# A triangular inverse kept in two shared PSUM banks, and GpSimd adding the squares of six row tiles

## The chip, the cores and the metric

The kernel runs on one core of a Trainium2 chip. The metric is the device time of one execution in microseconds (us). Each version is timed in several executions and the median is reported. One further execution is recorded by the hardware profiler; the line numbers, durations and waits below come from that one.

The engines of the core work side by side, each through its own fixed list of instructions, and wait for one another by semaphores: TensorE (PE, the matmuls; its weight loads are shown as PEld), VectorE (DVE), ScalarE (ACT), GpSimd (POOL) and SyncE (SP, which issues the DMAs). Operands lie in SBUF, or in PSUM, which the matmuls write.

## The reference

One inference step of a decoder with two layers, for a prompt of 512 tokens and 8 samples of 4 tokens, 544 token columns in all, at a model width of 1024. Layer 0 mixes tokens by dilated window attention, layer 1 by an RWKV-7 recurrence; both also attend to 256 memory tokens, are gated and go through an output projection. What matters here is layer 1:

```python
def step(S, inp):
    r_t, w_t, k_t, v_t, a_t, b_t = inp
    sa = jnp.einsum('bhvk,bhk->bhv', S, a_t)
    S = S * w_t[:, :, None, :] + sa[..., None] * b_t[:, :, None, :] + v_t[..., None] * k_t[:, :, None, :]
    return S, jnp.einsum('bhvk,bhk->bhv', S, r_t)
...
h = jnp.concatenate([y, o_mem], axis=-1) * jax.nn.silu(gate)
return h @ w_out, cols[:, -1], S.astype(xn.dtype)
...
xp = xp + rms_norm(hp, norm_post[i])
```

There are 12 heads of 64 channels. The last line, an RMS norm over the 1024 channels of the projection's output, is the end of the program: it needs the sum of the squares of all eight row tiles (8 x 128 channels).

## The kernel before, in words

**The recurrence in chunks.** The kernel takes the 512 prompt tokens in 8 chunks of 64. Heads go in pairs (six pairs p), and two pairs make a group g (three groups, 0 to 2). For each pair, coroutines called `decay`, `keys`, `receptance`, `values` and `scores` compute the scaled vectors and the masked score matrices (tiles `SA`, `SR`). For each group follow three serial steps:

- `products(g)` inverts, for each of 32 (head, chunk) units, a unit triangular 64x64 matrix. It is cut in 32x32 blocks; DVE lays them out so that each of the 128 partitions holds one 32x32 block, by a transpose into the SBUF tile `TT` (L1354), writes ones on the diagonal (L1355), and eliminates in 30 steps s = 1 to 30 (L1377 to L1382). Each step is two DVE instructions on s x (31-s) elements per partition: a product into the SBUF tile `TX` (L1380), and an addition of it into `TT` in place (L1382). The elements of a step depend on those of the step before. Two small squarings (after steps 5 and 12) serve the samples' small chunks. Then `TT` is transposed into `TX` (L1390), PE makes the off-diagonal blocks (tiles `X`, L1396 and L1405, with a second transpose at L1397 between them), and then the products called w, q and v.
- `recur(g)` runs the chain over the eight chunks. Its states and its z products lie in a PSUM tile that `ps_zs` gives out: 128 partitions x 1024 words, two banks, one buffer. The chain's last state is `St_7`, and it reports `end{g}` when done with the tile. The cross attention of layer 1 uses the same two banks ahead of group 0 and reports `cross`.
- `norm` and `sample` normalise the outputs y and treat the samples.

So the backbone of layer 1 is elimination, X, w/q/v, chain, then the next group's elimination. Beside it runs other work that fills the engines: the input projection of later pairs (PE matmuls `b_h`, three per product of high and low parts of the split numbers, L301 to L303), the splitting of weights (ACT `hi_...` L293, POOL `lo_...` L294), the gates (`u`, `gt`, L1131 to L1133), and the output projection (`outer`, PE matmuls `o`, with the gated vectors `ug` split into `h`, L1688 to L1690).

**The end.** `last(0)` and `last(1)` finish the projection for the 256 columns and the 288 columns of the tokens. For each of eight row tiles they run six matmuls, add them to `z` (DVE, L1722), square z (ACT, L1724, tiles `sqo`), and have PE sum the squares over partitions by products with a column of ones (`add_squares`, L316, tile `ssz`). Then comes the reciprocal root (L328 to L343, whose result for part 0 is `rs_p`), the scaling of z (L1733), the addition of the residual `xr` (L1734; three tiles on DVE, five on POOL), and the store.

**What sets the order.** Each stage is a coroutine; its `yield`s carry estimated times, or the name of an event that it must wait for. A small event queue in the kernel (`flow`) runs the coroutines in the order that these estimates and ranks give, and the framework's list scheduler then settles the order of every engine's instructions from a simulated timeline. A `yield` more, an instruction more or a buffer less moves the order of everything behind it. The list of each engine is then fixed.

```python
def add_squares(acc, sq, n, first, last): ...      # PE, L316
RADD = (0, 3, 6)                                   # rows whose residual DVE adds
LAT = [4.0, 5.82, 0.4, 0.6, 5.42, 5.2, 1.5, 0.94, 2.61, 0.6]
RANK = [4, 2, 7, 3, 2, 4, 6, 9]
```

Of the kernel before, what the change touches and what calls it, by code (L numbers as in the profile page):

```python
# [16 lines left out]
ALU = mybir.AluOpType  # L17
# [11 lines left out]
RAWO = 4  # L29
XRB = 8  # L30
OFF = {0: 0, 8: 0, 9: -200, 10: -200}
RADD = (0, 3, 6)
ET = mybir.EngineType
D, A, G = ET.DVE, ET.Activation, ET.Pool
# [134 lines left out]
class Flow:  # L169
# [29 lines left out]
    def run(self):  # L199
        while self.streams:  # L200
            s = self.pick()
            try:
                with self.tc.high_priority(OFF[s.rank]) if OFF.get(s.rank) else ExitStack():
                    r = next(s.gen)
# [21 lines left out]
def _device(tc, I, O):  # L226
    nc = tc.nc
# [31 lines left out]
    def ps_zs(name):  # L259
        return psum[0].tile([128, 1024], F32, tag="zs", bufs=1, name=name)  # L260
# [51 lines left out]
    def add_squares(acc, sq, n, first, last):  # L312

        for i in (0, 256, 128) if n > 256 else (0, 128):
            w = min(128, n - i)
            nc.tensor.matmul(acc[0:w, i // 128:i // 128 + 1], sq[:, i:i + w], ones[:, 0:1],  # L316
                             start=first and i == 0, stop=last and i == 128)
# [124 lines left out]
    with ExitStack() as pro:  # L442
        pm = pool(pro, "x", 1)
        for h in range(2):
            x = [pm.tile([128, 4, HF], F32, name=f"x{h}{i}") for i in range(2)]
            sq = []
# [24 lines left out]
        for h in range(2):  # L471
            acc = ps_q(f"ss0{h}")
# [181 lines left out]
    with ExitStack() as pro:  # L654
# [14 lines left out]
        for h in range(4):  # L669
            t = bd[h:h + 1, :]  # L670
# [203 lines left out]
    u = pb_pool.tile([128, 4, NT], F32, tag="PB", bufs=1, name="u0")  # L874
# [29 lines left out]
    def bank(h):  # L904
        return ps_c("so", "ssz1") if h else ps_o("ssz0")

    acc, rp, wo, wide, sums, lates, ready = [bank(0), bank(1)], [None, None], [], [], [], [], {}
# [434 lines left out]
    def products(g):  # L1342
# [7 lines left out]
        TT = rw.tile([128, 32, 32], F32, tag="TT", bufs=1, name=f"TT{g}")  # L1350
        TX = rw.tile([128, 32, 32], F32, tag="TX", bufs=1, name=f"TX{g}")
        N_ = SA[:, 0].rearrange("p j (c b t) -> p (j c) b t", b=2, t=32)
        flat = TX.rearrange("p u t -> p (u t)")
        nc.vector.transpose(TT.rearrange("p j t -> p t j"), N_.rearrange("p u b t -> p t b u"))  # L1354
        nc.vector.memset(TT.rearrange("p s t -> p (s t)")[:, 0:1024:33], 1.0)  # L1355

        ts = flat[:, 512:704].rearrange("p (k j t) -> p k j t", k=3, j=2)
        nc.vector.transpose(ts[:, 0], SAs)
        for r in Q0:
# [17 lines left out]
        for s in range(1, 31):  # L1377
            w = 31 - s
            pd = flat[:, 0:s * w].rearrange("p (j t) -> p j t", t=w)
            nc.vector.tensor_tensor(pd, TT[:, s:s + 1, s + 1:32].to_broadcast([128, s, w]),  # L1380
                                    TT[:, 0:s, s:s + 1].to_broadcast([128, s, w]), ALU.mult)
            nc.vector.tensor_tensor(TT[:, 0:s, s + 1:32], TT[:, 0:s, s + 1:32], pd, ALU.add)  # L1382
            if s in (5, 12):
                yield 0.0, LAT[9]
                square(s // 12)
                yield 0.2, LAT[9]
            else:
                yield 0.0, LAT[9]

        nc.vector.transpose(TX.rearrange("p u s -> p s u"), TT)  # L1390
        yield 0.0, LAT[6]

        pt = ps_q(f"X{g}1")
        for u in range(16):
            for a, b in zip(Q0, Q1):
                nc.tensor.matmul(pt[b, 32 * u:32 * u + 32], N_[a, u, 1], TX[a, u], start=True, stop=True)  # L1396
        nc.vector.transpose(N_.rearrange("p u b t -> p t b u"), TT.rearrange("p j t -> p t j"))  # L1397
        for hh, b in enumerate(Q1):
            nc.gpsimd.memset(N_[b, :, 0], 0.0)
            both[hh](TX[b, 0:16], pt[b].rearrange("p (u t) -> p u t", t=32))  # L1400
# [21 lines left out]
        u = st.u = UV[:, 0].rearrange("p j (c e v) -> p (j c) e v", c=4, e=2)  # L1422
# [278 lines left out]
    def last(i):  # L1701

        n, ts = (256, 288)[i], PART[i]
        z, h1 = out.z[i], out.h1
        t, xr = by_row(i, "SA", 2048, "xr1")
        m = 7 + (not i)
        nc.sync.dma_start(t[:, 0:m * n].rearrange("p (k t) -> p k t", t=n), x1d[:, 0:m, ts])
        if i:
            nc.sync.dma_start(xr[7], x1d[:, 7, ts])
        for j in (4, 5):  # L1710
            gated(j, (i,))
        yield 0.0, 2.0
        zs = ps_zs("ssz11") if i else None
        acc = zs[:, 0:512] if i else ps_t("ssz10")
        sqs = []
        for mt in range(8):
            ps = ps_mm(f"o2{mt}{i}")
            for k in range(2):
                a = (mt % 2 * 2 + k) * 128
                mm1(ps, out.w2h[:, mt // 2, a:a + 128], out.w2l[:, mt // 2, a:a + 128],  # L1720
                    h1[:, 0, 4 + k, ts], h1[:, 1, 4 + k, ts], n, k == 0, k == 1)
            nc.vector.tensor_tensor(z[mt], z[mt], ps[:, :n], ALU.add)  # L1722
            sq = tmp(f"sqo1{mt}{i}")[:, 0:n]
            nc.scalar.activation(sq, z[mt], AF.Square)  # L1724
            sqs.append(sq)
            if mt:
                add_squares(acc, sqs[mt - 1], n, mt == 1, False)
            yield 0.75, 0.2
        add_squares(acc, sqs[7], n, False, True)
        rp = rstd_of(acc, n, lambda name: zs[:, 512:1024] if i else ps_t(name), f"p1{i}")  # L1730
        yield 0.2, 2.0
        for kt in range(8):
            nc.vector.scalar_tensor_tensor(z[kt], z[kt], vec("post1", kt), rp, ALU.mult, ALU.mult)  # L1733
            (nc.vector if kt in RADD else nc.gpsimd).tensor_tensor(z[kt], z[kt], xr[kt], ALU.add)  # L1734
            nc.sync.dma_start(O["y"][:, kt, ts], z[kt])
            yield 0.0, 0.7
# [128 lines left out]
```

## Time and profile before

| what | value |
|---|---|
| median of 3 runs | 885.98 us (885.35 to 887.4) |
| the profiled execution | 886.03 us, of which the span from the first to the last instruction is 884.2 us |
| mean granted TensorE clock | 0.94 of full speed |
| PE / DVE / ACT / POOL busy | 91% / 60% / 34% / 39% of the span |
| elimination of group 0, 1, 2 (first L1380 to L1390) | 495.5 to 547.2, 612.9 to 663.7, 731.7 to 776.0 us |
| last chain state `St_7` of group 0, 1, 2 | 615.1, 727.7, 837.9 us |
| last matmul of `last(1)`'s sums of squares ends | 872.2 us |

A row of the timeline reads: start, duration, engine, line, operation, output <- inputs, shape (partitions x elements per partition), and how many alike follow each other (xN). A bracket gives the idle time before it and whose result ended it. The grouped view has, after the bar, the total busy time and the mean in ns. In the stretches view each engine's busy time in us is followed by its number of instructions, and PEclk is the clock that the throttle granted. The trace counts an fp32 matmul of sums (L316) as two instructions where the program has one.

### The profile page before, as it was taken

The page shows a single profiled execution, that of the slowest core. Times are in us where ns is not written, and L with a number is a line of the kernel's source. Part 1 is how long each engine was busy: PE and PEld are TensorE (multiplying, and loading weights), DVE is VectorE, ACT ScalarE, POOL GpSimd, SP SyncE. Part 2 cuts the span into 40 slices and gives each one's busy share as a digit, 9 for nine tenths or more (in the row PEclk, how much of TensorE's full clock was granted, in tenths as well). Part 3 has the DMA queues.
Part 4 walks back from the last instruction along what each step waited for, and adds up shares of the span by engine and source line. Part 5 has one row for each costly group of instructions (what it writes and reads, how often), then busy time and mean ns, then how long its engine had stood idle before and what let it go on. Part 6 is the DMA issues. An engine that isn't in the chain of part 4 may idle for free.

```text
span 884.2 us, 19847 instructions
## 1 busy us (share of the span) xinstructions
PE 805.3 (91%) x8144; PEld 685.6 (78%) x8144; DVE 529.5 (60%) x1189; ACT 304.9 (34%) x657; POOL 346.4 (39%) x426
## 2 busy tenths in 40 slices
PE   5799999999999988899999997998899898599984
PEld 4688777868876758898888876887688787389884
DVE  6534321256276356665775999567997569942563
ACT  6324321233254244455452343322433123222220
POOL 3543213311220335455542455353554344534432
PEclk9999999999999989899999998999999999589975
DMA  5461285672211664343133321201122212422011
GB/s 208 132 225 61 96 288 193 220 259 74 73 62 68 237 217 150 107 163 107 49 98 129 113 66 51 75 27 52 60 78 75 86 60 92 129 69 97 29 55 53
DMA packets 58510, 99.09 MB, mean 112 GB/s; under 512 B 6351, under 2 KB 24047, under 8 KB 58383
## 3 DMA queue, kind: packets, MB, share of 16 engines
q1 hardware_dynamic: 58420, 97.83, 33.5%
q8 instruction: 64, 1.05, 0.5%
q14 instruction: 26, 0.21, 0.1%
HBM read 83.76 MB, written 14.05 MB: 111 GB/s over the span
## 4 chain that ended last, share of the span: by engine, by line
PE 68%; DVE 19%; issue 5%; ACT 3%; DMA 2%; POOL 2%; DVEq 0%; SPq 0%; ACTq 0%; POOLq 0%
DVE TT L1382 3%; DVE TX L1380 3%; PE o L301 2%; PE o L302 2%; PE o L303 2%; PE o L746 2%; PE sc L1312 2%; PE so L830 2%; PE sA L775 1%; PE y L1566 1%; PE b_h L301 1%; PE z L1566 1%; PE pa L738 1%; PE b_h L302 1%; PE ssz L316 1%
## 5 line engine op out<-in xcount | busy, mean ns | idle before, releaser
L294 POOL TENSOR_TENSOR lo_a<-raw_a,hi_a 128x512 fp32r<-128x512 f32 x46 | 60.0, 1304 | 138.7 <-ACT hi_a L293 137.4
L294 POOL TENSOR_TENSOR lo_b<-raw_b,hi_b 128x512 fp32r<-128x512 f32 x58 | 77.3, 1334 | 59.4 <-ACT hi_b L293 54.2
L293 ACT CAST hi_b<-raw_b 128x512 fp32r<-128x512 f32 x58 | 35.8, 618 | 80.4 <-PE b_h L303 26.3
L293 ACT CAST hi_a<-raw_a 128x512 fp32r<-128x512 f32 x48 | 29.7, 619 | 67.2 <-issue 13.5
L301 PE MATMUL b_h<-xg,hi_b 128*128 128x272 f32 x160 | 48.8, 312 | 3.6 <-DVE C L1072 3.1
L303 PE MATMUL b_h<-xg,hi_b 128*128 128x272 f32 x160 | 47.2, 300 | 0.0
L302 PE MATMUL b_h<-xg,lo_b 128*128 128x272 f32 x160 | 47.1, 299 | 0.0
L1380 DVE TENSOR_TENSOR TX<-TT 128x30 f32<-128x30 f32 (+14 forms) x90 | 44.7, 497 | 1.7
L1382 DVE TENSOR_TENSOR TT<-TT,TX 128x30 f32<-128x30 f32 (+14 forms) x90 | 42.4, 471 | 1.7
L301 PEld LDWEIGHTS b_h<-xg,hi_b 128*128 128x128 f32 x160 | 31.0, 196 | 6.7 <-DVE C L1072 3.8
L303 PEld LDWEIGHTS b_h<-xg,hi_b 128*128 128x128 f32 x160 | 31.0, 194 | 1.0 <-issue 0.8
L302 PEld LDWEIGHTS b_h<-xg,lo_b 128*128 128x128 f32 x160 | 31.0, 195 | 0.8 <-issue 0.5
L1312 PE MATMUL sc<-AR,BK 64*64 64x128 f32 x384 | 26.9, 276 | 0.0
L301 PE MATMUL o<-h,hi_o1a 128*128 128x256 f32 (+1 forms) x64 | 20.1, 326 | 3.8 <-ACT h L1689 3.8
L1312 PEld LDWEIGHTS sc<-AR,BK 64*64 64x64 f32 x384 | 20.5, 133 | 3.1 <-issue 1.2
L1608 POOL TENSOR_TENSOR Sd<-St,DF 128x128 f32<-128x128 f32 x21 | 9.8, 468 | 32.6 <-DVE St L1624 31.7
L303 PE MATMUL o<-h,hi_o1a 128*128 128x256 f32 (+1 forms) x64 | 19.8, 324 | 1.3 <-POOL h L1690 1.3
L302 PE MATMUL o<-h,lo_o1a 128*128 128x256 f32 (+1 forms) x64 | 19.7, 320 | 0.0
L723 ACT ACTIVATE P<-P,m 128x768 f32<-128x768 f32 x16 | 15.0, 937 | 12.0 <-DVE m L722 11.9
L1221 POOL TENSOR_TENSOR rv<-rv,mhalf 128x10 f32<-128x10 f32 x6 | 11.8, 1959 | 18.2 <-DVE rv L1220 18.2
L301 PE MATMUL o<-h,hi_o1b 128*128 128x256 f32 (+1 forms) x32 | 11.4, 355 | 8.3 <-ACT h L1689 5.4
L746 PE MATMUL o<-PT,vt 128*64 128x128 f32 x192 | 17.6, 283 | 0.5 <-ACT PT L739 0.5
(915 smaller groups left out, 2869.6 us busy)
## 6 DMA issues: line engine op xcount, KB each, us to landing
raw_b<-in_w_in_b SPq DMA_DIRECT2D x58, 256.0 KB, 2.6
raw_a<-in_w_in_a SPq DMA_DIRECT2D x48, 256.0 KB, 2.7
kc<-in_kc SPq DMA_DIRECT2D x18, 512.0 KB, 5.2
vc<-in_vc SPq DMA_DIRECT2D x18, 512.0 KB, 4.7
out_win<-t SPq DMA_DIRECT2D x12, 272.0 KB, 2.1
PB<-bd SPq DMA_DIRECT2D x4, 576.0 KB, 7.2
x<-in_x SPq DMA_DIRECT2D x4, 544.0 KB, 6.0
xr<-in_x SPq DMA_DIRECT2D x16, 136.0 KB, 2.7
```

What stands on the lines that cost most here:

```text
L293: nc.scalar.copy(hi, raw)
L294: lo_eng.tensor_tensor(lo, raw, hi.bitcast(F32), ALU.subtract)
L301: nc.tensor.matmul(ps[:, :n], hi, xh, start=first, stop=False)
L302: nc.tensor.matmul(ps[:, :n], lo, xh, start=False, stop=False)
L303: nc.tensor.matmul(ps[:, :n], hi, xl, start=False, stop=last)
L723: nc.scalar.activation(P, P, AF.Exp, bias=m1[:, 0:1], scale=1.0, accum_out=m1[:, 1:2])
L746: nc.tensor.matmul(po[64 * hh:64 * hh + 64, 0:128], v, PT[hh][:, j, :], start=j == 0, stop=j == 5)
L830: nc.tensor.matmul(po[QD[b4], 0:256], PT[:, 4 * j + k, QD[b4]], vc[b4][:, k, :], start=j + k == 0, stop=False)
L1312: nc.tensor.matmul(pt[unit(c, j, h)[0], a:a + 128], BK[H2[h], j, x, CH[c]], AR[H2[h], j, :, CH[c]], start=True, stop=True)
L1380: nc.vector.tensor_tensor(pd, TT[:, s:s + 1, s + 1:32].to_broadcast([128, s, w]), TT[:, 0:s, s:s + 1].to_broadcast([128, s, w]), ALU.mult)
L1382: nc.vector.tensor_tensor(TT[:, 0:s, s + 1:32], TT[:, 0:s, s + 1:32], pd, ALU.add)
L1566: nc.tensor.matmul(out, lhs, rhs, start=start, stop=stop)
```

## The change

Three edits.

1. In `products`, after `TT` is transposed and its diagonal set, the coroutine waits for `end{g-1}` (`cross` for group 0), takes the two banks of `ps_zs` as a tile `TP` (the rows below call it T), and ACT copies `TT` into it in two halves of 128x512 (new line L1361). The elimination's running matrix is now `TP` in PSUM. The product reads one operand from `TP` and the row s from `TT`, which is still in SBUF and no longer written; the addition reads and writes `TP` and takes the product from `TX` in SBUF.
2. The two transposes behind the elimination read `TP`.
3. In `last`, POOL adds the squares of row tiles 1 to 5 into those of tile 0 (new L1734); PE sums over partitions only tile 6, that sum, and tile 7. In the program that is 25 matmul instructions fewer: 10 in part 0 (16 to 6) and 15 in part 1 (24 to 9).

```diff
+SQ1 = 6
...
+        yield f"end{g - 1}" if g else "cross"
+        TP = ps_zs(f"T{g}")
+        for h in range(2):
+            nc.scalar.copy(TP[:, 512 * h:512 * h + 512], TT[:, 16 * h:16 * h + 16].rearrange("p s t -> p (s t)"))
+        TP = TP.rearrange("p (s t) -> p s t", t=32)
...
-            nc.vector.tensor_tensor(pd, TT[:, s:s + 1, s + 1:32].to_broadcast([128, s, w]),
-                                    TT[:, 0:s, s:s + 1].to_broadcast([128, s, w]), ALU.mult)
-            nc.vector.tensor_tensor(TT[:, 0:s, s + 1:32], TT[:, 0:s, s + 1:32], pd, ALU.add)
+            nc.vector.tensor_tensor(pd, TP[:, 0:s, s:s + 1].to_broadcast([128, s, w]),
+                                    TT[:, s:s + 1, s + 1:32].to_broadcast([128, s, w]), ALU.mult)
+            nc.vector.tensor_tensor(TP[:, 0:s, s + 1:32], TP[:, 0:s, s + 1:32], pd, ALU.add)
...
-        nc.vector.transpose(TX.rearrange("p u s -> p s u"), TT)
+        nc.vector.transpose(TX.rearrange("p u s -> p s u"), TP)
...
-        nc.vector.transpose(N_.rearrange("p u b t -> p t b u"), TT.rearrange("p j t -> p t j"))
+        nc.vector.transpose(N_.rearrange("p u b t -> p t b u"), TP.rearrange("p j t -> p t j"))
...
-            if mt:
-                add_squares(acc, sqs[mt - 1], n, mt == 1, False)
+            if 0 < mt < SQ1:
+                nc.gpsimd.tensor_tensor(sqs[0], sqs[0], sq, ALU.add)
+            if mt > SQ1:
+                add_squares(acc, sqs[mt - 1], n, mt == SQ1 + 1, False)
             yield 0.75, 0.2
+        add_squares(acc, sqs[0], n, False, False)
         add_squares(acc, sqs[7], n, False, True)
```

The line numbers behind the first edit move by one, those behind the elimination by eight on the whole (L1380 becomes L1387, L1382 L1389, L1390 L1397, L1131 L1132), and those in and behind `last` by seven to ten (L1688 to L1695, L1722 to L1729, L1733 to L1743). The order of all engines from some 490 us on is another. Three places show what the prediction speaks of.

**DVE, group 2's elimination.** Before, from its third step on (L1461 to L1468 are the norm of group 1, `u` the gates):

```order
L1380 TENSOR_TENSOR TX_8324<-TT_8323 128x84
L1462 SCALAR_TENSOR_TENSOR yc_8_8049<-gst_8_8048,y_4_7874 128x512
L1382 TENSOR_TENSOR TT_8323<-TT_8323,TX_8324 128x3x28
L1380 TENSOR_TENSOR TX_8324<-TT_8323 128x108
L1382 TENSOR_TENSOR TT_8323<-TT_8323,TX_8324 128x4x27
L1465 TENSOR_REDUCE gst_8_8048<-y_8_8050 128x8
L1380 TENSOR_TENSOR TX_8324<-TT_8323 128x130
L1131 SCALAR_TENSOR_TENSOR u_8787<-b_h_8800,rs_83 128x272
L1466 TENSOR_SCALAR gst_8_8048<-gst_8_8048 128x8
L1382 TENSOR_TENSOR TT_8323<-TT_8323,TX_8324 128x5x26
```

After, from the transpose into TT to the first half of the third step:

```order
L1355 STREAM_TRANSPOSE TT_8329<-SA_7437 128x32x32
L1327 TENSOR_TENSOR SAs_7442<-sc5s,mks 128x32
L1327 TENSOR_TENSOR SRs_7443<-sc5s,mks 128x32
L1631 TENSOR_TENSOR St_7_8019<-z_7657,Sd_7_7999 128x128
L1566 MEMSET St2i 128x128
L1356 MEMSET TT_8329 128x32
L1365 STREAM_TRANSPOSE TX_8330<-SAs_7442 128x64
L1387 TENSOR_TENSOR TX_8330<-T_8333,TT_8329 128x30
L1389 TENSOR_TENSOR T_8333<-T_8333,TX_8330 128x30
L1387 TENSOR_TENSOR TX_8330<-T_8333,TT_8329 128x58
L1389 TENSOR_TENSOR T_8333<-T_8333,TX_8330 128x2x29
L1387 TENSOR_TENSOR TX_8330<-T_8333,TT_8329 128x84
```

The transpose into TT now stands ahead of the chain's last state St_7, not behind it, and the gates (`u`), which stood between the steps of this elimination, stand ahead of it, among those of group 1 and its chain. From the transpose into TT to the one into TX, DVE has beside the elimination 56 instructions of other work before and 65 after in group 0, 60 and 80 in group 1, 34 and 29 in group 2.

**ACT, the copies of group 2.** The same stretch of its list, after:

```order
L1696 CAST h_9460<-ug_9474 128x544
L1696 CAST h_9460<-ug_9479 128x544
L1361 COPY T_8333<-TT_8329 128x512
L1296 COPY UV_7439<-av_8296 128x512
L1361 COPY T_8333<-TT_8329 128x512
L1296 COPY UV_7439<-av_8303 128x512
L294 CAST w2h<-raw_o1c_9499 128x512
```

Two copies are new; one copy of UV stands between them, and casts for the output projection stand ahead. The first step of the elimination waits for ACT.

**DVE and POOL, between the two last parts.** DVE before:

```order
L328 TENSOR_SCALAR rv_p_10007<-ssz_9910 128x2
L1488 SCALAR_TENSOR_TENSOR bv_7389<-gn2s,pv,bv_7389 128x32
L1488 SCALAR_TENSOR_TENSOR bv_8195<-gn2s,pv,bv_8195 128x32
L1688 SCALAR_TENSOR_TENSOR ug_9900<-bv_7389,pv,ug_9900 128x288
L1688 SCALAR_TENSOR_TENSOR ug_9905<-bv_8195,pv,ug_9905 128x288
L1733 SCALAR_TENSOR_TENSOR z_9485<-z_9485,pv,rs_p_10013 128x256 x8
L1734 TENSOR_TENSOR z_9485<-z_9485,xr_9898 128x256 x2
L1722 TENSOR_TENSOR z_9486<-z_9486,o_10051 128x288
```

DVE after:

```order
L1743 SCALAR_TENSOR_TENSOR z_9494<-z_9494,pv,rs_p_10017 128x256 x2
L1495 SCALAR_TENSOR_TENSOR bv_7395<-gn2s,pv,bv_7395 128x32
L1495 SCALAR_TENSOR_TENSOR bv_8201<-gn2s,pv,bv_8201 128x32
L1743 SCALAR_TENSOR_TENSOR z_9494<-z_9494,pv,rs_p_10017 128x256 x6
L1744 TENSOR_TENSOR z_9494<-z_9494,xr_9907 128x256
L1695 SCALAR_TENSOR_TENSOR ug_9909<-bv_7395,pv,ug_9909 128x288
L1695 SCALAR_TENSOR_TENSOR ug_9914<-bv_8201,pv,ug_9914 128x288
L1744 TENSOR_TENSOR z_9494<-z_9494,xr_9907 128x256 x2
L1729 TENSOR_TENSOR z_9495<-z_9495,o_10055 128x288
```

POOL after:

```order
L330 TENSOR_TENSOR rv_p_10011<-rv_p_10011,mhalf 128x2
L1744 TENSOR_TENSOR z_9494<-z_9494,xr_9907 128x256 x5
L1697 TENSOR_TENSOR h_9460<-ug_9909,h_9460 128x288
L1697 TENSOR_TENSOR h_9460<-ug_9914,h_9460 128x288
L1734 TENSOR_TENSOR sqo_10063<-sqo_10063,sqo_10073 128x288
L1734 TENSOR_TENSOR sqo_10063<-sqo_10063,sqo_10084 128x288
```

The gated vectors ug of part 1, from which the h of `last(1)` is made, now stand behind all eight scalings of part 0 on DVE, and the h on POOL behind its five residual additions; before they stood ahead of both.

On PE the projection matmuls that fill the backbone's gaps move between stages. Of the 3312 of L301 to L303, 2289, 2700 and 2989 came before X of group 0, 1 and 2, and 2515, 2917 and 3234 before the last z of the three chains; after, it is 2317, 2797 and 3034, and 2489, 2941 and 3240.

## The prediction

> **What bounds the kernel now.** I read the page first: its busy shares, its chain of work that ended last, and the two costliest DVE groups.
>
> ```profile
> span 884.2 us, 19847 instructions
> PE 805.3 (91%) x8144; PEld 685.6 (78%) x8144; DVE 529.5 (60%) x1189; ACT 304.9 (34%) x657; POOL 346.4 (39%) x426
> PE 68%; DVE 19%; issue 5%; ACT 3%; DMA 2%; POOL 2%; DVEq 0%; SPq 0%; ACTq 0%; POOLq 0%
> DVE TT L1382 3%; DVE TX L1380 3%; PE o L301 2%; PE o L302 2%; PE o L303 2%; PE o L746 2%; PE sc L1312 2%; PE so L830 2%; PE sA L775 1%; PE y L1566 1%; PE b_h L301 1%; PE z L1566 1%; PE pa L738 1%; PE b_h L302 1%; PE ssz L316 1%
> ...
> L1380 DVE TENSOR_TENSOR TX<-TT 128x30 f32<-128x30 f32 (+14 forms) x90 | 44.7, 497 | 1.7
> L1382 DVE TENSOR_TENSOR TT<-TT,TX 128x30 f32<-128x30 f32 (+14 forms) x90 | 42.4, 471 | 1.7
> ```
>
> PE carries 68% of the chain, but DVE's largest pieces in it are the two lines of the elimination: 180 instructions, 44.7 + 42.4 = 87.1 us. The profiled execution took 886.03 us, 0.05 above the median of the runs (885.98), so sums made against it hold for the median. Next I read the timeline of DVE in group 2's elimination, with POOL beside it.
>
> ```profile
> 744.08 0.87 DVE L1488 SCALAR_TENSOR_TENSOR bv<-gn,pv,bv 128x256 f32<-128x256 f32 x2
> 744.38 1.28 POOL L294 TENSOR_TENSOR lo_o1a<-raw_o1a,hi_o1a 128x512 fp32r<-128x512 f32 x1 [3.22 <-ACT hi_o1a L293]
> 744.87 1.02 DVE L1382 TENSOR_TENSOR TT<-TT,TX 128x210 f32<-128x210 f32 x1
> ...
> 755.40 0.41 DVE L1382 TENSOR_TENSOR TT<-TT,TX 128x240 f32<-128x240 f32 x1
> ...
> 761.85 3.31 POOL L1690 TENSOR_TENSOR h<-ug,h 128x544 fp32r<-128x544 f32 x2 [1.41 <-ACT h L1689]
> 762.44 1.52 DVE L1380 TENSOR_TENSOR TX<-TT 128x210 f32<-128x210 f32 x1
> ...
> 765.43 0.37 DVE L1380 TENSOR_TENSOR TX<-TT 128x198 f32<-128x198 f32 x1
> ...
> 773.29 0.24 DVE L1382 TENSOR_TENSOR TT<-TT,TX 128x84 f32<-128x84 f32 x1
> ```
>
> An instruction of the elimination takes 0.37 us at 198 elements and 1.52 at 210. The long one begins while POOL runs (its two from 761.85 to 765.16); at 765.43, with POOL idle, the next step is short. The one at 744.87 is held to 745.89, and POOL runs until 745.66. The two bv instructions ahead of it, which read gn from PSUM and so have only one large SBUF input, are not held: 0.87 us for two of 128x256, although POOL has started before the second. **A DVE instruction with two SBUF inputs is held by a running POOL instruction; one with a PSUM input isn't.**
>
> Clean, an instruction takes 0.24 us at 84 elements and 0.41 at 240, so about 0.15 + 0.00109 n. The 30 steps have s(31-s) elements, 4960 in all, done twice: 60 x 0.15 + 9920 x 0.00109 = 19.8 us for a group, 59.4 us for three. 87.1 - 59.4 = **some 28 us are stall**, about 9 a group.
>
> Then the stretches, to see what the stall is worth where it lies. The first is group 0's elimination, the second its X, products and chain; the next two the same of group 1, the next two of group 2; then the tail.
>
> ```profile
> core 0: us, PE busy (x) PEld busy (x) DVE busy (x) ACT busy (x) POOL busy (x), PEclk, DMA share, GB/s
> 495.00:551.00 56.00, 49.26 (x379) 42.26 (x378) 54.81 (x120) 23.61 (x47) 27.99 (x47) 0.94 0.20 65
> 551.00:613.00 62.00, 59.73 (x1105) 52.20 (x1104) 37.84 (x87) 16.72 (x35) 27.03 (x39) 1.00 0.17 54
> 613.00:664.00 51.00, 44.23 (x372) 38.50 (x370) 49.78 (x119) 19.84 (x41) 25.46 (x34) 0.97 0.19 61
> 664.00:729.00 65.00, 60.39 (x1106) 54.15 (x1104) 39.25 (x84) 16.63 (x35) 25.27 (x28) 0.95 0.22 73
> 729.00:776.00 47.00, 31.13 (x252) 25.23 (x248) 44.96 (x98) 13.47 (x27) 23.65 (x22) 0.73 0.37 111
> 776.00:840.00 64.00, 64.00 (x1049) 58.20 (x1049) 24.98 (x52) 15.64 (x34) 24.65 (x27) 0.96 0.20 65
> ...
> 856.00:872.00 16.00, 16.00 (x82) 15.76 (x80) 2.88 (x7) 3.10 (x7) 0.00 (x0) 0.53 0.09 30
> ```
>
> In each elimination DVE is busy to within 2.1 us of the stretch, so DVE sets its length. But PE is close behind: idle 6.7, 2.3, 6.8, 4.6, 15.9 and 0 us, 36 in all. PE's work up to there isn't reduced, so the gain can't exceed these 36 us and what a higher clock would give in group 2's elimination (31.13 us at 0.73; at 0.96 they would be 23.7, so 7 more).
>
> **The change part by part.**
>
> *The elimination in PSUM.* Each product and each addition now has one input in PSUM and one in SBUF. By the bv rows the stalls go. What an instruction costs then is bounded by rows of equal size:
>
> ```profile
> L1722 DVE TENSOR_TENSOR z<-z,o 128x256 f32<-128x256 f32 x8 | 3.3, 420 | 2.9 <-PE o L303 2.8
> L1468 DVE TENSOR_TENSOR yc<-yc,gst 128x256 f32<-128x256 f32 x2 | 0.8, 422 | 0.1
> L293 ACT CAST hi_b<-raw_b 128x512 fp32r<-128x512 f32 x35 | 21.6, 617 | 43.4 <-PE b_h L303 24.6 <-issue 9.0 <-PE b17h L303 4.7
> L1295 ACT COPY UV<-av 128x512 f32<-128x512 f32 x10 | 5.8, 587 | 16.1 <-PE av L1288 9.6 <-PE av L1294 6.4
> ```
>
> With one input in PSUM (o) 420 ns, with both in SBUF 422: no difference for a read. No DVE instruction of this trace writes PSUM, and none reads there what the one before wrote. From below I allow 0.03 us an instruction gained, from above the fixed 0.15 once more (the whole trip paid twice). I take 0, as the rows that are nearest have it.
>
> [...]
>
> *The moved work.* The elimination's two lines group by group (0, 1, 2):
>
> ```profile
> L1380 DVE TENSOR_TENSOR TX<-TT 128x30 f32<-128x30 f32 (+14 forms) x30 | 16.3, 543 | 0.6
> L1382 DVE TENSOR_TENSOR TT<-TT,TX 128x30 f32<-128x30 f32 (+14 forms) x30 | 12.9, 430 | 0.5
> L1380 DVE TENSOR_TENSOR TX<-TT 128x30 f32<-128x30 f32 (+14 forms) x30 | 14.0, 467 | 0.5
> L1382 DVE TENSOR_TENSOR TT<-TT,TX 128x30 f32<-128x30 f32 (+14 forms) x30 | 13.7, 456 | 0.6
> L1382 DVE TENSOR_TENSOR TT<-TT,TX 128x30 f32<-128x30 f32 (+14 forms) x30 | 15.8, 528 | 0.6
> L1380 DVE TENSOR_TENSOR TX<-TT 128x30 f32<-128x30 f32 (+14 forms) x30 | 14.4, 479 | 0.6
> ```
>
> They sum to 29.2, 27.7 and 30.2 us. DVE's other instructions in these stretches then have a mean of (54.81 - 29.2)/60 = 0.43 us in group 0, 0.37 in group 1 and 0.39 in group 2. The order adds 9, 20 and -5 of them: +3.9, +7.5, -2.0. The stall taken out is 29.2 - 19.8 = 9.4, 7.9 and 10.4. So DVE has 5.5 us less in group 0's stretch, about as much as before in group 1's, and 12.4 less in group 2's, where the transpose into TT (2.2 us) also moves ahead of the chain's end.
>
> PE's filling moves too. At 0.125 us a matmul (L301 to L303 back to back at full clock), 28 more ahead of X of group 0 are +3.5 us; 54 fewer from there to St_7 of group 0 are -6.8; 123 more in group 1's elimination +15.4; 73 fewer in its chain -9.1; 21 more in group 2's +2.6; 39 fewer behind it -4.9. Taking in each stretch the longer of the two engines:
> - group 0's elimination: DVE -5.5, PE has 6.7 - 3.5 to give: **-3**
> - its X and chain, PE full: **-6**
> - group 1's elimination: PE 44.2 + 15.4 = 59.6 against 51: **+9**
> - its X and chain: **-9**
> - group 2's elimination: DVE 47 - 12.4 - 2.2 = 32.4, PE 31.1 + 2.6 = 33.7: **-13**
> - its X and chain: **-5**
>
> Together -27 of the 36 us that PE has idle.
>
> *Two ACT copies per group.* 0.59 us each, by the UV copies of the same size; one other copy and the queue stand ahead or between. DVE's transpose of SAs (0.2 us) and another two instructions cover a part; I take 1.5 us in groups 0 and 2, nothing in group 1 (there PE sets the pace): **+3**. If ACT stands on a cast whose buffer PE must free, it is more; the waits of L293 on PE are 24.6 us over 35 casts, 0.7 each on the mean. The wait for `end{g-1}` holds the copies until St_7 is made, and the 1.5 us of group 2 begin there. Behind the waiting copies on ACT stand a copy of UV and the casts of w2h, for which PE's w products and projection wait; both are wanted only after the elimination or have other matmuls ahead of them, so I cost that wait at nothing, and at one copy (0.59 us) a group where it shows.
>
> POOL's work stays; its instructions now hold DVE's other ones with two SBUF inputs more often. I take **+2** for that.
>
> *The tail.* Before:
>
> ```profile
> 849.11 0.94 DVE L1688 SCALAR_TENSOR_TENSOR ug<-bv,pv,ug 128x288 f32<-128x288 f32 x2
> 850.31 3.22 DVE L1733 SCALAR_TENSOR_TENSOR z<-z,pv,rs_p 128x256 f32<-128x256 f32 x8 [0.26 <-PE rs_p L343]
> ...
> 851.68 3.83 POOL L1734 TENSOR_TENSOR z<-z,xr 128x256 f32<-128x256 f32 x5
> ...
> 855.35 0.40 PE L301 MATMUL o<-h,w2h 128*128 128x288 f32 x1 [1.95 <-DVE z L1722]
> ...
> 858.44 1.13 PE L316 MATMUL ssz<-ones,sqo 128*128 128x1 f32 x6
> 859.44 0.59 PE L301 MATMUL o<-h,w2h 128*128 128x288 f32 x1
> 862.02 0.59 PE L301 MATMUL o<-h,w2h 128*128 128x288 f32 x1
> ...
> 868.76 3.41 PE L316 MATMUL ssz<-ones,sqo 128*128 128x1 f32 x18
> ```
>
> PE sets the pace at half clock (0.53 above): 2.58 us a row tile, of which 1.0 is a square's sum (858.44 to 859.44). Four such stand between rows and go, -4.0 us; three remain, as many as in the 3.41 us at the end. POOL's sums (0.8 us a row, as its 3.83/5 shows) lie beside rows of 1.58. Against this, ug now stands behind six scalings and an addition (some 3.2 us on DVE), and h on POOL behind five additions. PE's first row then starts near 854, where before two rows were done and PE waited until 855.35 for DVE. Eight rows at 1.58 and 3.41 us end at 870.0, with the first two at full clock at 868.5, all at full clock at about 862.3; before at 872.17. I take **-4**, and behind it all stays.
>
> Sum: -27 + 3 + 2 - 4 = -26; I round to -25, so **861 us**.
>
> **The rivals.**
> 1. *An access to PSUM is dearer*, because each step reads what the one before wrote there. At a third of the fixed 0.15 us an instruction, 180 of them are 9 us; two groups of three show it: +6 to +8, **868**. For it: nothing in the trace has this form. Against: reads are equal.
> 2. *PE becomes the bound and doesn't give back.* Group 1's elimination grows by 9 us, and the chains behind, serial in PE, DVE and POOL, shorten by only half of what their filling loses. The sum is then -3 - 3 + 9 - 4.5 - 13 - 2.5 = -17, + 5 - 4: **870**. For it: PE at 91%.
> 3. *Slower: the fixed cost in PSUM doubles.* From 0.16 us an instruction (28/180) the stall's gain is gone. The ACT copies and the fuller group 1 then stay as a loss: +3 + 2 + 9 - 4, less what group 2's moved work gives (-4): **about 892**. Against: equal reads; for: the in-place column access is in no row.
> 4. *The stall isn't what it seems*, and the elimination stays at 29 us a group: copies +3, tail -4, **885**. Against: every long one I looked at ends with POOL's. [...]
> 5. *Better*: the tail's denser matmuls get the full clock (-10 in place of -4) and the clock of group 2's stretch rises: **850**.
>
> **How the numbers follow.** Forecast 861 (853 to 867) 0.48; rival 1 0.18; rival 2 0.18; rival 3 0.07; rival 4 0.04; rival 5 0.05. The range 847 to 879 takes in the forecast, rivals 1, 2 and 5 with their own spread and leaves out 3 and 4 and the outer ends of the others: about 0.8 is inside. A measurement of this kernel can tell some 0.2% (1.8 us) from no change: faster 0.89, same 0.04, slower 0.07.
>
> **What would show it.** The elimination's two lines: 180 instructions at a sum near 60 us, with none above 0.5 us (forecast), 69 (rival 1), 87 (3, 4). The stretches: group 2's elimination from its first step to its last transpose near 32 to 34 us instead of 44.3 (731.7 to 776.0), group 1's as long or longer with PE near 100%. The tail: row tiles of 0.8 or 1.6 us, not 2.58. It is wrong if ACT's copies land much later than the transpose into TT, or if other DVE instructions take over the stalls.

## The result and the profile after

The changed kernel takes 864.35 us (median of 4 runs, 859.73 to 867.57) against 886.69 for the kernel before beside it: a ratio of 0.9748, 95% interval 0.9723 to 0.9774, so 22.3 us less. Beside the later experiments it was timed again: 859.56 against 886.3, ratio 0.9703 (0.9679 to 0.9727). The forecast was 861.

The page of the changed kernel (profiled execution 866.0 us), the lines that answer to those shown of before:

```profile
span 864.2 us, 19767 instructions
PE 792.4 (92%) x8094; PEld 670.6 (78%) x8094; DVE 506.6 (59%) x1189; ACT 306.6 (35%) x663; POOL 354.2 (41%) x436
...
PE 75%; DVE 13%; POOL 4%; DMA 3%; issue 3%; ACT 3%; DVEq 0%; SPq 0%; POOLq 0%; ACTq 0%
PE o L302 2%; PE b_h L302 2%; PE b_h L303 2%; PE b_h L304 2%; PE o L303 2%; PE o L747 2%; PE o L304 2%; PE so L831 2%; PE sA L776 2%; PE sc L1313 2%; PE y L1573 1%; PE pa L739 1%; PE lo L1192 1%; PE z L1573 1%; PE ox L561 1%
```

DVE's share of the chain fell from 19 to 13%, and the elimination's lines are no longer in the list. The grouped view of DVE has them (busy us and mean ns behind the bar, then idle time ahead of them):

```profile
L1389 DVE TENSOR_TENSOR T<-T,TX 128x30 f32<-128x30 f32 (+14 forms) x90 | 29.9, 332 | 1.6
L1387 DVE TENSOR_TENSOR TX<-T,TT 128x30 f32<-128x30 f32 (+14 forms) x90 | 29.2, 324 | 4.1 <-ACT T L1361 2.5
```

59.1 us where there were 87.1. The longest of the 180 takes 0.42 us; before, 30 of them took over 0.5. The largest shape, 240 elements, has these means:

```profile
L1389 DVE TENSOR_TENSOR T<-T,TX 128x240 f32<-128x240 f32 x6 | 2.5, 409 | 0.1
L1387 DVE TENSOR_TENSOR TX<-T,TT 128x240 f32<-128x240 f32 x6 | 2.4, 393 | 0.0
```

And the timeline of DVE in group 2's elimination, with POOL's row of the same time:

```profile
754.89 0.38 DVE L1387 TENSOR_TENSOR TX<-T,TT 128x228 f32<-128x228 f32 x1
755.20 0.20 DVE L1381 COPY TX<-n 32x64 f32<-32x64 f32 x1
755.33 0.38 DVE L1389 TENSOR_TENSOR T<-T,TX 128x228 f32<-128x228 f32 x1
755.74 0.39 DVE L1387 TENSOR_TENSOR TX<-T,TT 128x220 f32<-128x220 f32 x1
756.16 0.40 DVE L1389 TENSOR_TENSOR T<-T,TX 128x220 f32<-128x220 f32 x1
...
755.22 2.65 POOL L1697 TENSOR_TENSOR h<-ug,h 128x544 fp32r<-128x544 f32 x2
```

POOL runs from 755.22 to 757.87, and the steps beside it take 0.38 to 0.40 us. Before, a step beside the same line of POOL took 1.52.

Where the time went, by stages. Each stage runs from the event named to the next; "again" is the profiled execution of the second timing, 859.96 us:

| stage (us) | before | changed | again | change | forecast |
|---|---|---|---|---|---|
| start to the transpose into TT of group 0 | 492.1 | 496.1 | 490.5 | +4.0 / -1.6 | 0 |
| to X of group 0 | 59.1 | 56.8 | 56.8 | -2.4 | -3 |
| to St_7 of group 0 | 63.8 | 59.2 | 59.2 | -4.6 | -6 |
| to X of group 1 | 51.5 | 56.9 | 56.8 | +5.4 | +9 |
| to St_7 of group 1 | 61.2 | 64.4 | 64.2 | **+3.1** | **-9** |
| to X of group 2 | 53.8 | 36.7 | 35.9 | **-17.5** | -13 |
| to St_7 of group 2 | 56.5 | 55.1 | 55.1 | -1.4 | -5 |
| to the end | 46.3 | 39.3 | 39.2 | **-7.0** | -4 |
| span | 884.2 | 864.2 | 857.6 | -20.0 / -26.6 | -25 (with +3 and +2 for copies and stalls) |

(The change's column takes the mean of the two where they differ by less than 1 us.)

The first row isn't the change's. The code up to there is the same; in the first profiled execution PE had a stretch at less than full clock there that the other two don't have (and from 350 to 400 us a clock of 0.86 where they have 0.92 and 0.93). The stretch from 100 to 150 us, before and changed:

```profile
100.00:150.00 50.00, 50.00 (x359) 36.91 (x356) 10.93 (x25) 10.50 (x23) 12.15 (x17) 1.00 0.70 233
```

```profile
100.00:150.00 50.00, 50.00 (x341) 38.16 (x342) 9.57 (x24) 9.87 (x22) 10.95 (x14) 0.93 0.68 214
```

The other rows rest on single executions too. In group 1's chain the execution before had a granted clock of 0.95 (664 to 729 us); two of the kernels below, e1 and e9, run the same list of instructions there and take 57.4 us where the table has 61.2. The stage in e1, at a granted clock of 1.00:

```profile
669.40:726.90 57.50, 53.89 (x1073) 48.23 (x1072) 34.47 (x76) 14.11 (x30) 22.64 (x24) 1.00 0.23 79
```

Set against 57.4, that chain became 6.9 us longer, not 3.1. The other stages of layer 1 in e1 and e9 differ from the column "before" by at most 1.6 us, so differences of that size say little.

### The profile page after: what moved, and what is told of

It reads as the page before. It is cut to its first block, busy times and chain, and to the rows that moved or that the text cites. A ratio compares the mean times of both kernels' runs of the same rounds, so it can differ in the third digit from the quotient of the medians.

```text
span 864.2 us, 19767 instructions
## 1 busy us (share of the span) xinstructions
PE 792.4 (92%) x8094; PEld 670.6 (78%) x8094; DVE 506.6 (59%) x1189; ACT 306.6 (35%) x663; POOL 354.2 (41%) x436
## 4 chain that ended last, share of the span: by engine, by line
PE 75%; DVE 13%; POOL 4%; DMA 3%; issue 3%; ACT 3%; DVEq 0%; SPq 0%; POOLq 0%; ACTq 0%
PE o L302 2%; PE b_h L302 2%; PE b_h L303 2%; PE b_h L304 2%; PE o L303 2%; PE o L747 2%; PE o L304 2%; PE so L831 2%; PE sA L776 2%; PE sc L1313 2%; PE y L1573 1%; PE pa L739 1%; PE lo L1192 1%; PE z L1573 1%; PE ox L561 1%
## 5 line engine op out<-in xcount | busy, mean ns | idle before, releaser
L302 PE MATMUL b_h<-xg,hi_b 128*128 128x272 f32 x160 | 46.8, 300 | 0.4 <-DVE u L1132 0.4
L303 PE MATMUL b_h<-xg,lo_b 128*128 128x272 f32 x160 | 46.3, 297 | 0.0
L304 PE MATMUL b_h<-xg,hi_b 128*128 128x272 f32 x160 | 45.5, 293 | 0.0
L302 PEld LDWEIGHTS b_h<-xg,hi_b 128*128 128x128 f32 x160 | 29.7, 188 | 3.3 <-issue 0.9
L1387 DVE TENSOR_TENSOR TX<-T,TT 128x30 f32<-128x30 f32 (+14 forms) x90 | 29.2, 324 | 4.1 <-ACT T L1361 2.5
L1389 DVE TENSOR_TENSOR T<-T,TX 128x30 f32<-128x30 f32 (+14 forms) x90 | 29.9, 332 | 1.6
L303 PEld LDWEIGHTS b_h<-xg,lo_b 128*128 128x128 f32 x160 | 29.8, 188 | 1.3 <-issue 0.7
L304 PEld LDWEIGHTS b_h<-xg,hi_b 128*128 128x128 f32 x160 | 29.6, 188 | 0.4
L1313 PE MATMUL sc<-AR,BK 64*64 64x128 f32 x384 | 24.5, 276 | 0.1
L302 PE MATMUL o<-h,hi_o1a 128*128 128x288 f32 (+1 forms) x64 | 20.3, 323 | 1.6 <-ACT h L1696 1.6
L303 PE MATMUL o<-h,lo_o1a 128*128 128x288 f32 (+1 forms) x64 | 19.6, 318 | 0.0
L304 PE MATMUL o<-h,hi_o1a 128*128 128x256 f32 (+1 forms) x64 | 19.5, 317 | 0.1
L740 ACT COPY PT<-pa 128x512 f32<-128x512 f32 x16 | 9.3, 584 | 22.6 <-PE pa L739 18.4
L1222 POOL TENSOR_TENSOR rv<-rv,mhalf 128x10 f32<-128x10 f32 x6 | 11.7, 1952 | 13.5 <-DVE rv L1221 13.5
```

Source lines behind the costliest of these rows:

```text
L302: nc.tensor.matmul(ps[:, :n], hi, xh, start=first, stop=False)
L303: nc.tensor.matmul(ps[:, :n], lo, xh, start=False, stop=False)
L304: nc.tensor.matmul(ps[:, :n], hi, xl, start=False, stop=last)
L1313: nc.tensor.matmul(pt[unit(c, j, h)[0], a:a + 128], BK[H2[h], j, x, CH[c]], AR[H2[h], j, :, CH[c]], start=True, stop=True)
L1387: nc.vector.tensor_tensor(pd, TP[:, 0:s, s:s + 1].to_broadcast([128, s, w]), TT[:, s:s + 1, s + 1:32].to_broadcast([128, s, w]), ALU.mult)
L1389: nc.vector.tensor_tensor(TP[:, 0:s, s + 1:32], TP[:, 0:s, s + 1:32], pd, ALU.add)
```

## The experiments

The nine kernels below ran beside the kernel before in three sittings; ratios are to the kernel before of the same sitting, with the 95% interval.

| run | median us | before, us | ratio |
|---|---|---|---|
| e1_squares_only | 877.22 | 884.83 | 0.9913 (0.9883 to 0.9944) |
| e2_psum_only | 862.67 | 884.83 | 0.9765 (0.9705 to 0.9824) |
| e3_product_in_psum | 868.30 | 884.83 | 0.9820 (0.9786 to 0.9854) |
| e4_ug_ahead_tail | 857.51 | 884.83 | 0.9685 (0.9665 to 0.9704) |
| e5_ug_behind_state | 855.20 | 886.30 | 0.9657 (0.9623 to 0.9692) |
| e6_both_moves | 854.47 | 886.30 | 0.9651 (0.9619 to 0.9682) |
| e7_product_psum_squares | 859.29 | 886.30 | 0.9704 (0.9677 to 0.9731) |
| e8_changed_again | 859.56 | 886.30 | 0.9703 (0.9679 to 0.9727) |
| e9_squares_in_a_batch | 883.40 | 885.10 | 0.9966 (0.9939 to 0.9994) |

### Is it the second SBUF input? (e3)

Theory: a DVE instruction with two SBUF inputs is held by a running POOL instruction. The rivals: any contact with PSUM makes these instructions shorter, or the stall has another cause. The kernel before, with the product going to PSUM; the matrix stays in SBUF:

```diff
+        yield f"end{g - 1}" if g else "cross"
+        PD = ps_zs(f"T{g}")
...
-            pd = flat[:, 0:s * w].rearrange("p (j t) -> p j t", t=w)
+            pd = PD[:, 0:s * w].rearrange("p (j t) -> p j t", t=w)
```

> The kernel before, with one alteration: the product of each elimination step goes to PSUM (the two shared banks, with the wait for their release) and not to TX; the running matrix stays in SBUF. The product still has two SBUF inputs, the addition has one in SBUF and one in PSUM. Theory (a DVE instruction with two SBUF inputs is held by a running POOL instruction): the product's line stays near 40 to 45 us, the addition's falls from 42 to 30. Rival (PSUM makes every one of them shorter, or the shorter chain does): both fall to 30. Rival (the stall has nothing to do with inputs): both stay near 43. By the theory the time falls by about half of what the elimination in PSUM brings, 875 to 882.

The two lines (the PSUM tile is T here):

```profile
L1382 DVE TENSOR_TENSOR T<-TT 128x30 f32<-128x30 f32 (+14 forms) x90 | 46.7, 519 | 1.7
L1384 DVE TENSOR_TENSOR TT<-TT,T 128x30 f32<-128x30 f32 (+14 forms) x90 | 29.0, 322 | 1.7
```

The product, still with two SBUF inputs, takes 46.7 us, and writing to PSUM doesn't help it; the addition, with one, falls from 42.4 to 29.0. That is what the theory said, and neither rival. The time fell by more than expected (875 to 882): 16.5 us for 11.4 us of stall taken out (87.1 - 75.7). There are no ACT copies here, and the engines' order is another too, though PE's projection matmuls lie nearly as before (2294, 2688 and 2994 of them ahead of the three X). The stage from X to St_7 of group 0 became 5.7 us shorter, though the elimination doesn't lie in it; why wasn't separated. (Group 1's reads 3.3 us shorter, 57.9 us, which is about what e1 and e9 have.)

### The two halves of the change (e1, e2)

e1 is the kernel before with the third edit alone, e2 the changed kernel with that edit undone:

```diff
-            if mt:
-                add_squares(acc, sqs[mt - 1], n, mt == 1, False)
+            if 0 < mt < SQ1:
+                nc.gpsimd.tensor_tensor(sqs[0], sqs[0], sq, ALU.add)
+            if mt > SQ1:
+                add_squares(acc, sqs[mt - 1], n, mt == SQ1 + 1, False)
```

> Only the third edit (GpSimd adds six row tiles' squares; the elimination stays in SBUF). The order of the engines up to the last projection is that of before, and the two ug of the last part stand ahead of the scalings, as before. Theory (the squares' sums are on PE's path there): the four gaps of 1.0 us between row tiles go, so -4 us, 882; if the denser matmuls also get the full clock, rows of 0.8 us in place of 1.58, -9 us, 877. Rival (the sums are hidden or POOL's additions become the bound): within 2 us of before, 885 to 888.

> Only the first two edits (elimination in PSUM; the squares as before). [...] Rival (most of the gain of the change is from the tail): 878 or more.

e1 gained 7.6 us, by the second branch of its theory: the clock rises. The last stage (St_7 of group 2 to the end) is 37.7 us against 46.3. Its stretches, then those of before, with PE's busy time behind the length of the stretch and the granted clock third from the end:

```profile
854.00:858.00 4.00, 4.00 (x24) 4.00 (x24) 1.50 (x4) 1.46 (x4) 2.08 (x4) 0.71 0.26 86
858.00:862.00 4.00, 3.11 (x25) 2.70 (x24) 1.12 (x4) 1.20 (x3) 1.54 (x3) 1.00 0.00 0
```

```profile
857.00:862.00 5.00, 5.00 (x24) 4.94 (x25) 0.91 (x2) 1.07 (x3) 0.00 (x0) 0.50 0.12 41
862.00:867.00 5.00, 5.00 (x25) 4.94 (x25) 0.91 (x2) 0.73 (x3) 0.00 (x0) 0.50 0.00 0
867.00:872.00 5.00, 5.00 (x26) 4.91 (x26) 0.45 (x1) 0.86 (x2) 0.00 (x0) 0.50 0.00 0
```

Before, PE was busy for all of 15 us and stayed at half clock; without the sums it came to full clock within the part.

e2 gained 22 us, 5 us beyond the range expected (868 to 873), but its runs scatter (860.18 to 872.16), and the profiled one is the slowest. There the tail is as in the kernel before (46.1 us, row tiles 2.58 apart, 847.19, 849.76, 852.34). The two halves do not add up: 7.6 and 22.2 us alone, 22.3 or 26.7 together. One cause is shown by e4 below (in the changed kernel the last part starts late; in e2 it doesn't). Some 5 us of the profiled execution's excess lie ahead of the change (495.7 us to the transpose into TT of group 0, 490.5 in the changed kernel's second profile). Whether the other cause is that e2's faster executions, whose mean clock is 0.953 to 0.959 against 0.946 in the profiled one, had a faster clock in the tail stays open, since they have no trace. So what the third edit adds to the other two is shown by the tail of the profiled executions alone (46.1 against 39.2 us), not by the times: e2's interval reaches to those of the changed kernel.

### What held the last part (e4)

In the changed kernel's order ug and h of the last part stand behind the scalings and additions of part 0. Its timeline:

```profile
834.28 0.44 PE L344 MATMUL rs_p<-ident,rvx_p 128*128 128x128 f32 x2 [0.68 <-ACT rvx_p L337]
840.31 0.85 PE L302 MATMUL o<-h,w2h 128*128 128x288 f32 x2 [5.28 <-ACT h L1696]
...
835.87 2.43 DVE L1743 SCALAR_TENSOR_TENSOR z<-z,pv,rs_p 128x256 f32<-128x256 f32 x6
838.82 1.40 DVE L1695 SCALAR_TENSOR_TENSOR ug<-bv,pv,ug 128x288 f32<-128x288 f32 x2
```

PE waits 5.28 us for h. In e4 dependencies put ug and h first, and part 0's three DVE additions behind the first z of the last part:

```diff
+            for j in (4, 5):
+                gated(j, (1,))
+            ends = [flow.last(e).name for e in (ET.DVE, ET.Pool)]
         for kt in range(8):
             nc.vector.scalar_tensor_tensor(z[kt], z[kt], vec("post1", kt), rp, ALU.mult, ALU.mult)
+            if not i:
+                tc.add_manual_dep(flow.last(ET.DVE), ends[0], SYNC, reason="order")
+            if not i and kt in RADD:
+                out.late.append((z[kt], xr[kt], O["y"][:, kt, ts]))
+                continue
```

> The changed kernel, with the two ug of the last part and their h put ahead of the eight scalings of part 0 on DVE and of its residual additions on POOL, and part 0's three DVE additions behind the first z of the last part. Theory (the changed order holds PE for 5.3 us before the last part because h comes late): PE starts the last part 4 to 5 us earlier, and the program ends 3 to 4 us earlier than the changed kernel, about 861. Rival (the first z then waits behind the scalings, as in the kernel before): nothing gained, 864.

```profile
831.09 0.85 PE L302 MATMUL o<-h,w2h 128*128 128x288 f32 x2 [1.40 <-ACT h L1696]
```

PE's wait fell from 5.28 to 1.40 us, and the last stage from 39.2 to 36.1. The median is 857.51, 2 to 7 us below the changed kernel's two; the interval of its ratio overlaps that of e8, so the size is 3 us by the traces and not settled by the times.

### What held the second chain (e5)

The forecast had the stage from X to St_7 of group 1 9 us shorter; it became 3 longer. DVE there, in the changed kernel:

```profile
721.00 0.29 DVE L1631 TENSOR_TENSOR St<-z,Sd 128x128 f32<-128x128 f32 x1 [0.65 <-PE z L1573]
721.20 0.87 DVE L1495 SCALAR_TENSOR_TENSOR bv<-gn,pv,bv 128x256 f32<-128x256 f32 x2
726.05 0.79 DVE L1695 SCALAR_TENSOR_TENSOR ug<-bv,pv,ug 128x544 f32<-128x544 f32 x1 [3.98 <-issue]
...
728.21 1.67 DVE L1695 SCALAR_TENSOR_TENSOR ug<-bv,pv,ug 128x544 f32<-128x544 f32 x1
...
731.07 2.15 DVE L1355 STREAM_TRANSPOSE TT<-SA 128x1024 f32<-128x1024 f32 x1
...
733.24 0.28 DVE L1631 TENSOR_TENSOR St<-z,Sd 128x128 f32<-128x128 f32 x1
```

```profile
728.35 0.46 PE L1573 MATMUL z<-UV,BK 64*64 64x64 f32 x16
```

The last two states of the chain (721.00 and 733.24) are 12 us apart. Between them DVE stands still for 4 us at a ug that isn't there yet, with the chain's own instructions queued behind. The z that St_7 needs is done at 728.8; St_7 comes 4.4 us later, as a ug and the transpose into TT stand ahead of it. The view names no releaser for the 4 us ("issue"), but SyncE's queue has the store and the loads that fit, and the last line has the times from issue to landing of the eight loads:

```profile
718.85 0.33 SPq L1139 DMA_DIRECT2D ud<-u  x1
...
721.03 8.61 SPq L1691 DMA_DIRECT2D ug<-ud  x3
...
DMA to landing us min/median/max: 2.7/2.9/4.6
```

The last of the eight gates goes out to memory at 718.85 and has landed at 720.97. Only then does SyncE issue the load of the first ug that DVE needs (721.03; it brings back an earlier gate). The trace has it land at 725.62, 4.6 us after its issue and the longest of the eight, and the ug starts at 726.05. Before, the first ug stood in group 2's elimination (760.20), and DVE had no idle time ahead of any of the eight; the new order puts this wait for memory in the chain, as the gates moved ahead. In e5 the four ug wait for St_7 of group 1:

```diff
+        if g == 1:
+            out.st7 = step.name
...
+            if len(parts) == 2:
+                tc.add_manual_dep(flow.last(ET.DVE), out.st7, SYNC, reason="order")
```

> The changed kernel, with the ug of the first four row blocks put behind the last state St_7 of the second chain on DVE (before, one of them holds DVE for 4.0 us in that chain while it waits for its load from memory, and St_7 stands behind it). Theory (this wait is why the second chain became 3 us longer and not 9 shorter): St_7 comes 5 to 7 us earlier than in the changed kernel, the elimination behind it as much, and the program ends 3 to 6 us earlier, 858 to 861, if the projection's matmuls that need these h find room in the last elimination. Rival (PE has as much to do behind it): St_7 earlier, the end within 2 us of the changed kernel.

> Both moves of ug together: behind the second chain's last state, and ahead of the scalings in the last part. Theory: the two gains lie in different stages and add up, so 4 us below e4_ug_ahead_tail (857.5) if the former brings 4: 851 to 855. Rival: 857.

```profile
721.76 0.25 DVE L1631 TENSOR_TENSOR St<-z,Sd 128x128 f32<-128x128 f32 x1
```

St_7 of group 1 comes at 721.76, in e8, which starts the stages at the same time, at 727.46: 5.7 us earlier, and the stage is 58.5 us where before it took 61.2 (57.4 in e1 and e9). X of group 2 begins 4.6 us earlier, the span is 6.7 us shorter; the medians differ by 4.4 (855.20 against 859.56, same sitting). The theory holds. e6, with both moves, came out at 854.47, inside the range of its theory, but it is no faster than e5 alone: the two gains don't add up. e5's order says why in part. There the ug of the last part already stand ahead of the scalings, because the dependency shifted the rest of the list:

```
L1697 SCALAR_TENSOR_TENSOR ug_9909<-bv_7395,pv,ug_9909 128x288
L1697 SCALAR_TENSOR_TENSOR ug_9914<-bv_8201,pv,ug_9914 128x288
...
L1747 SCALAR_TENSOR_TENSOR z_9494<-z_9494,pv,rs_p_10017 128x256 x8
```

So in e5 and e6 PE starts the last part as early behind the last St_7 (11.3 us) as in e4 (11.5; 15.5 in e8). But then it waits for a z on DVE, here in e5, then in e6:

```profile
829.24 0.61 PE L302 MATMUL o<-h,w2h 128*128 128x288 f32 x1 [3.93 <-DVE z L1733]
```

```profile
829.06 0.61 PE L302 MATMUL o<-h,w2h 128*128 128x288 f32 x1 [3.15 <-DVE z L1735]
```

Behind this wait its matmuls come at half clock (one every 0.24 us) until the sixth (e5) or seventh row tile (e6), where e4 has the full clock from the fourth. The last stage takes 40.1 and 39.6 us, against 36.1 in e4, so what e4 gained there is in neither; that the wait is the cause was not tried. e5 and e6 are the fastest kernels of this study, some 31 us below the kernel before.

### Do the parts add up when ug is in time? (e7, e8)

e7 is e3 with the squares on GpSimd and e4's order of the last part.

> The product of each step in PSUM and the matrix in SBUF, as in e3_product_in_psum (no ACT copies), with GpSimd adding the squares and ug ahead of the scalings in the last part. Theory (the two edits lie in different stages, and add up when ug isn't late): 868.3 less 8 to 11, 857 to 860. Rival (they share a gain, as the squares brought nothing beside the elimination in PSUM): 865 or more.

859.29, as the theory had it: by the ratios 1.2% below e3, and the last stage is 36.3 us where e3 has 46.1. Less than half of the stall taken out (11.4 of 28 us), without ACT copies, gives as much here as all of it with the changed kernel's order (e8); but e7 also has e4's order of the last part, which e8 lacks.

> The changed kernel unaltered, beside the others on this chip: 860 to 866, with the spread between its runs from a stretch of half clock of PE in the first 490 us, which the change leaves alone: runs without it near 860 to 862, runs with it 4 us above.

All four runs lie between 858.43 and 860.81, a little under the range.

### Why the clock stays low in the tail (e9)

e9 is the kernel before, with as much work on PE: the sums of the first five row tiles are held back until the sixth tile's matmuls are done.

```diff
+            if i and mt == 5:
+                end = flow.last().name
+                for k in range(5):
...
+                        tc.add_manual_dep(flow.last(), end, SYNC, reason="order")
```

> The kernel before, with no work taken off PE: in the last part the sums of squares of the first five row tiles are held back until the sixth tile's matmuls are done, so that six tiles' matmuls follow each other without sums between them. Theory (the sums of one column between the tiles, beside their own 1.0 us, keep PE's granted clock at half): the clock rises within two to three tiles, the later tiles take 0.8 us and a tile's sum 0.57, and the program ends 3 to 5 us earlier than before, 881 to 883. Rival (the sums cost only their own time): the clock stays at 0.50, and the time is that of before within 1 us, since as many sums remain.

PE in e9: the start of the third row tile, two matmuls of the fifth, the sums behind the sixth (18 of the batch's 30 instructions; the list scheduler put the others behind the seventh and eighth), and the start of the seventh tile. Then the granted clock of the stretches up to the fifth tile and from there to the sums:

```profile
855.64 0.61 PE L301 MATMUL o<-h,w2h 128*128 128x288 f32 x1 [1.95 <-DVE z L1722]
...
859.34 0.29 PE L301 MATMUL o<-h,w2h 128*128 128x288 f32 x1
859.47 0.29 PE L302 MATMUL o<-h,w2l 128*128 128x288 f32 x1
...
860.53 2.12 PE L1732 MATMUL ssz<-ones,sqo 128*128 128x1 f32 x18
862.51 0.47 PE L301 MATMUL o<-h,w2h 128*128 128x288 f32 x1
862.77 0.44 PE L302 MATMUL o<-h,w2l 128*128 128x288 f32 x1
```

```profile
855.60:859.20 3.60, 3.56 (x15) 3.56 (x16) 1.58 (x4) 1.34 (x3) 0.21 (x1) 0.50 0.51 168
859.20:860.50 1.30, 1.30 (x11) 1.30 (x11) 0.64 (x2) 0.44 (x1) 0.00 (x0) 0.99 0.00 0
```

The matmuls come every 0.24 us from 855.64, every 0.13 from 859.2, and every 0.24 again after 2 us of sums. So the sums between the tiles do hold the clock down, beside their own time. The last stages of all profiles agree: 46.0 to 46.3 us with the sums between the rows (before, e2, e3), 36.1 to 40.1 without them (the changed kernel, e1, e4 to e8), 42.6 in e9. Of the whole time the gain is 0.34% (0.06 to 0.61), 1.7 us between the medians: the sign of the theory, with a size that the times leave open, as the batch itself sends the clock back. The rival falls by the clock, not by the time.

## Why the forecast was right, step by step

- **The stall.** Worked out: 59.4 us for the 180 instructions without it. Measured: 59.1. The cause is shown by e3.
- **PSUM at no extra price.** Of the range from -0.03 to +0.15 us an instruction the value taken, 0, is the one that was measured: 0.39 and 0.41 us in the mean at 240 elements, where a clean instruction before took 0.41. The additions also write PSUM, where the next instructions read it; the 180 took 59.1 us, against 59.4 worked out from clean steps in SBUF. Rivals 1, 3 and 4 fell with these two numbers.
- **DVE sets groups 0 and 2, PE group 1.** Group 0: -2.4 against -3; both engines are nearly full there (in the second profile PE 55.1 and DVE 53.9 of 56.7 us), so which of them sets it isn't shown. Group 1: +5.4 against +9, with PE full (56.5 of 56.9 us). Group 2: DVE's length was forecast at 32.4 us, and from the chain's last state (733.24) to the transpose into TX (765.61) it is 32.4. In part that is luck: the wait for the ACT copies, which the forecast booked apart, is in it. From the first step (735.45), as the forecast's sign had it, it is 30.2 us against 44.3. PE's 33.7, which I took as the bound, wasn't one: in this stretch it was busy for 21.3 of 33 us.

```profile
733.00:766.00 33.00, 21.31 (x172) 16.11 (x171) 27.84 (x90) 8.73 (x19) 12.59 (x13) 0.65 0.26 75
```

- **The ACT copies.** Forecast +3; DVE's idle time ahead of the elimination that ends with them is 2.5 us, in groups 0 and 2 (0.9 and 1.6), as forecast.
- **Stalls passed on.** Forecast +2; DVE's other instructions take 447.5 us (506.6 - 59.1) where they took 442.4. That is 5 us of busy time; what of it ended anything wasn't tried.
- **The second chain, where the sum failed.** "its X and chain: -9" is the term that was wrong by 12 us. The order listing showed the gates moving ahead, and I priced them as DVE and PE time only. The load behind the ug that moved with them wasn't followed through SyncE's queue. Of the 12 us this wait and its ug are 5.7 (e5); without them the stage is 2.7 shorter than in the profile before (and 1.1 longer than in e1 and e9), so the filling that left it (-9) was over-priced too. And the transpose into TT (2.2 us) was taken off the stage behind, but not added here, where it now stands ahead of St_7. The stage behind was under-priced by 4 to 5 us, and the third chain over-priced by 3.6.
- **Rival 2, PE doesn't give back.** On the chains it came nearer than the forecast. The three together became 2.9 us shorter, where the forecast had 20 and the rival 10; without the ug in the way (e5) 11.8. The eliminations became 14.5 us shorter where 7 was forecast. All six stages together: -17.4 us, between the forecast's -22 (with copies and stalls) and the rival's -12. Why the chains give back so little wasn't tried beyond e5.
- **The tail, mis-sized.** Forecast -4, measured -7. The late ug was forecast and is there (5.3 us of idle PE), the four sums too. What was left to rival 5 (0.05) is the clock: from the fourth tile on a row took 0.8 us, as the starts of the fourth and fifth show.

```profile
845.29 0.29 PE L302 MATMUL o<-h,w2h 128*128 128x288 f32 x1
846.09 0.31 PE L302 MATMUL o<-h,w2h 128*128 128x288 f32 x1
```

From its first row to the end of the sums PE took 11.7 us where it took 22.0, and the first row starts 15.4 us behind St_7 where it was 12.2: the late start took back 3.1 of 10.4 us.

That the total came out near the forecast owes something to luck, to errors of opposite sign: 12 us in the second chain and 3.6 in the third that didn't come, against 4.5 more than forecast in the stage of group 2's elimination, 3.6 us that group 1's took less, and 3 more in the tail. The mechanism and its size, the stall and its 28 us, did hold.

## What to carry to other kernels

Where short DVE instructions with two SBUF inputs run beside GpSimd, compare the same shape with GpSimd idle and running (before, at 210 elements, 0.38 and 1.52 us). The long ones ended with GpSimd's here, and moving one of the two inputs into PSUM took the stall out (the addition in e3, 42.4 to 29.0 us), while moving the output there did not (the product in e3, 46.7 us where it took 44.7). When a change shifts a scheduled order, follow every instruction that moved back to its load: the ug that wait for memory had no idle time of DVE ahead of them in one stage, and 4.0 us in the serial chain. And single-column matmuls between dense ones can cost more than their own time: with the same sums, those of five tiles held back, e9's dense matmuls came every 0.13 us from 859.2 to 860.5, where those of before came every 0.24.

## What the runs showed of the hardware that was not expected

PE was busy, as the profile counts it, 5.00 of 5.00 us three times over at a granted clock of 0.50 (kernel before, 857 to 872 us) while single-column sums stood between the row tiles. With dense tiles alone the matmuls from the third tile on also came every 0.24 us at first, for 1.1 us in the changed kernel (from 843.86), 3.6 in e9 (855.64), 4.5 in e1 (851.83), 5.2 in e5 (829.24) and 5.9 in e6 (829.06), and then every 0.13. In the kernel before the third tile had one every 0.13 (855.35 to 856.25); behind the first sums they came every 0.24 from 857.2 to the end of the last tile. And DVE instructions that add in place in PSUM, each reading what the one before wrote, take what they take in SBUF (0.41 us at 240 elements in both).
